# A two-layer transformer block: a fourth half-weight buffer in layer 0's MLP, casts in the order of the products, and modulation rows at 2 turns in 5

## The chip, the core and the metric

One core of a Trainium2 chip runs the whole program in one launch. TensorE (PE) multiplies, VectorE (DVE), ScalarE (ACT) and GpSimd (POOL) do the elementwise work, SyncE (SP) issues nearly all the DMAs, in order, on one queue. The metric is the device time of an execution in microseconds (us). Of the kernel before there are three runs, and one more execution was profiled.

## The reference

The program computes two layers over 512 latent tokens (model width 1024) that are conditioned by a vector c, with 256 context tokens beside them. Layer 0 mixes tokens by windowed grouped-query attention, layer 1 by differential attention, and each is followed by a squared-ReLU MLP of width 4096. Everything is float32.

```python
for i in range(DEPTH):
    mod_x = jax.nn.silu(c) @ w_ada[i] + b_ada[i]
    mod_c = jax.nn.silu(c_ctx) @ w_ada[i] + b_ada[i]
    sh1, sc1, g1, sh2, sc2, g2 = jnp.split(mod_x[:, None, :], N_MOD, axis=-1)
    ...
    x = layer_norm(alpha * x + g1 * ax, ln1_g[i], ln1_b[i])
    fx = sqrelu_mlp(x * (1.0 + sc2) + sh2, mlp_w1[i], mlp_w2[i])   # square(relu(h @ w1)) @ w2
    x = layer_norm(alpha * x + g2 * fx, ln2_g[i], ln2_b[i])
    if need_ctx:      # layer 0 only: the context tokens too
        ...
```

In layer 0 the MLP runs on 768 tokens (latents and context), in layer 1 on 512. The vectors sh, sc and g of both layers are the modulation; their weights, w_ada, are about 50 MB, of which much is loaded and multiplied on DVE while the MLP of layer 0 runs on TensorE.

## The kernel before, in words

**Products.** A float32 weight is split into a high part (ACT casts it to float32r) and a low part (DVE subtracts the high part from the float32 value), and so is each activation. `mm3` (lines 325 to 327) makes a product from three matmuls: high by high, high by low, low by high. So each weight needs a load, a cast on ACT and a subtraction on DVE before TensorE can use it.

**The MLP's first product** (`mlp_pipe`). The 4096 hidden features are taken in pairs of 256, q from 0 to 15. From pair 3 on a pair is done by seven products in place of eight, on quarters of the weights (a scheme like Strassen's). `part_sums` loads the pair's two weight tiles a1 and a2 (tiles `w_raw`, 128 x 1024, from in_w1), whose halves are A11, A12 and A21, A22, has POOL make the sums S1, S2, S3 and S4 from them (`w_sum`, or in place in `w_raw`), and splits A11, A12, A22 and the four sums into high and low parts: `half`, which writes a tile `w_half`, 128 x 1024, the high part left and the low part right. So a pair has seven halves. `weights(q, n)` asks for the first n of them; four of the next pair's are asked for by `ahead` in the middle of a pair, the other three when it starts.

`pair` then runs the products, TensorE in the order A11, A12, S2, S1, S3, S4, A22 (in layer 0 `p3_first` is true). Between them `mix` lets groups of the second product go (`y_groups`, accumulating in `y_ps`, weights `w_h` and `w_l` from in_w2, asked for by `y_weights`; 12 matmuls a group, six from each of two weight tiles). ACT copies a product's result to `relu` and DVE adds to it; product S4 accumulates on the buffer z that the add after S3 (`d3`, DVE `relu<-h_ps`) has to have read first. At a pair's end `squared` makes relu and square on ACT, and the result `hid` is split on ACT and DVE.

**Buffers in layer 0** (`R0`). A half's tile comes from `half_tile`: in turn one of the tiles of the w2 weights' high parts (tag wh), of their low parts (wl), and of the tag bc (two tiles, one of which holds `w_sum`). The ring `rhalf` of 3 says how many may be out. a1 and a2 have one tile each for all pairs, so the next pair's load of a2 waits until A22 is split, that of a1 until S4 is. The tiles `w_raw` of everything else, w2 weights and the modulation's w_ada (`in_w_adaT`), come in turn from NRAW = 3 tiles with the tag raw. Layer 1 (`R1`) has a ring of 4 and tiles of its own.

**Modulation rows.** The generator `filler` (`ada_rows`) does one row block a step: a load of 512 KB from in_w_adaT, then two multiply-and-sum operations on DVE (the CUSTOM operation `w_raw<-w_raw,cB` or `ada_pr<-w_raw,cB`). It has 58 steps. `extra` is called after each y group and once in `ahead`, 13 times in a pair, and takes a step at every third call. What is left at the end of layer 0 is done there. Gates made from them are transposed on TensorE (`gate_t`), copied by ACT (`gate_s`) and written to memory by SP (`gate_d`).

**The order.** Instructions are emitted by a list scheduler (`fl`), which runs the generators of the stages side by side by due times that it keeps itself; a wait in the hardware arises where an emitted instruction needs something later than expected. Each engine takes its instructions in the order emitted; SP's DMAs too, so a load that waits for a tile holds up all those behind it.

Of the kernel before, what the change touches and what calls it, by code (L numbers as in the profile page):

```python
# [15 lines left out]
AF = mybir.ActivationFunctionType  # L16
ALU = mybir.AluOpType
# [217 lines left out]
def hybrid_block(ctx: ExitStack, tc: tile.TileContext, t: dict, out: bass.AP):  # L235
# [460 lines left out]
    def mlp_pipe(l, hx, ready, ntok, acc, get_gates, done, fx, T, R):  # L696
# [40 lines left out]
        def part_sums(q):  # L737
            (a1, g1, f1), (a2, g2, f2) = R.pair_raws()
            q1 = dma(1024, [g1], out=a1, in_=t["w1"][l, 2 * q])
            q2 = dma(1024, [g2], out=a2, in_=t["w1"][l, 2 * q + 1])  # L740
            ws = R.sum_tile()
            (a11, a12), (a21, a22), (s3, s2) = [(x[:, 0:512], x[:, 512:1024]) for x in (a1, a2, ws)]

            def half(src, dep):
                nhalf[0] += 1
                w = R.half_tile(nhalf[0])
                a = ac(512, [dep, R.rhalf.get()], nc.scalar.copy, out=w[:, 0:512], in_=src)
                d = dv(512, [a], nc.vector.tensor_tensor, out=w[:, 512:1024], in0=src, in1=f(w)[:, 0:512],
                       op=ALU.subtract)
                rel = Task()  # L750
                rel.ring = R.rhalf
                return Weight(w[:, 0:512], w[:, 512:1024], d, rel)

            def add(o, x, y, op, deps):
                return gp(pool2(512), deps, nc.gpsimd.tensor_tensor, out=o, in0=x, in1=y, op=op)

            yield half(a11, q1)
            w12 = half(a12, q1)
            yield w12
            e3 = add(s3, a11, a21, ALU.subtract, [q1, q2])  # L760
            e1 = add(a21, a21, a22, ALU.add, [e3])
            e2 = add(s2, a21, a11, ALU.subtract, [e1])
            yield half(s2, e2)
            yield half(a21, e1)
            yield half(s3, e3)
            w = half(a22, q2)
            w.t.ring = f2
            yield w
            w = half(a12, add(a12, a12, s2, ALU.subtract, [e2, w12.t]))
            w.t.ring = f1  # L770
            yield w

        def squared(q, fi, r, d, c):
# [75 lines left out]

        def pair(q, mix, ahead):  # L850
            weights(q, 7 - len(Wp.get(q, [])))
            A11, A12, S2, S1, S3, A22, S4 = Wp[q]
            hid[q] = R.hid_tile(q)
            yield sS.ok
            X, slot = psS("h_ps")[:, 0:nh], sS.take()
# [21 lines left out]
            d3 = dv(nh, [p5, a3], nc.vector.tensor_tensor, out=r1[:, t2], in0=z, in1=r1[:, t2], op=ALU.add)  # L877
            ahead()
            yield from mix(2)
            yield [d3, S4.t if R.p3_first else A22.t]  # L880

            def p3():
                p = product(z, S4, lower(t2, 4), False)
                d = dv(nh, [p, a2], nc.vector.tensor_tensor, out=r0[:, t2], in0=z, in1=r0[:, t2], op=ALU.add)
                sm_.give(zs, d)
                squared(q, 0, r0, [d], slice(0, ntok))

            def p4():
                p = product(X, A22, whole(3), False)
                a = ac(nh, [p], nc.scalar.activation, out=r1[:, t1], in_=X, func=AF.Relu)  # L890
                sS.give(slot, a)
                squared(q, 1, r1, [a, d3], t2)

            if R.p3_first:
                p3()
                yield [a3, A22.t, Tr[3]]
                p4()
            else:
                yield [a3, A22.t, Tr[3]]
                p4()  # L900
                yield [d3, S4.t]
                p3()
            yield from mix(3)

        gates, st, Wy, fresh = [], {}, {}, set()
# [131 lines left out]
        else:  # L1037
# [4 lines left out]
            for _ in sums:  # L1042
                pass
        y_weights(0, 0)
        weights(3, 4)
        y_weights(0, 1, R.ahead)
        yield from steps(2 * ntb)
        for q in range(3, 16):
            if q == R.gate_at:
                gates += yield from get_gates()  # L1050
            if q == 4 and l == 0:
                st2["second"] = True

            def ahead():
                weights(q + 1, 4)
                if q < 14:
                    y_weights((q - 1) // 2, (q - 1) % 2, R.ahead)
                elif l or q == 15:
                    y_weights(6, 1, R.ahead)
                if q == 15:  # L1060
                    R.tail()
                R.extra()
            m = R.mixes[q < 14]
            if q < 15:
                y_weights((q - 2) // 2, q % 2)
            yield from pair(q, lambda i: steps(m[i]), ahead)
# [394 lines left out]
    with tc.tile_pool(name="mlp0", bufs=1, reuse_waits="tile") as pool:  # L1461
# [24 lines left out]
            fl.add(ln_job(pool, acc[tb], tb, hx, A, B, ready, st, r, fx[tb]), 0)  # L1486

        class R0:
            rhalf = Ring(fl, 3)
            mixes = ((2, 2, 2, 0), (4, 4, 4, 0))  # L1490
            p3_first, gate_at, res = True, 16, None
            ahead, done, turn = 1, 0, 0

            def pair_raws(self):
# [3 lines left out]
                return self.ws  # L1498

            def half_tile(self, n):  # L1500
                p_, tag, b = ((wpool, "wh", NH), (wpool, "wl", NH), (pool, "bc", 2))[n % 3]
                return p_.tile([P, 1024], F32R, name="w_half", tag=tag, bufs=b)

            def relu_tile(self):
# [21 lines left out]

            def extra(self):
                self.turn += 1
                if self.turn % 3 == 0:
                    next(filler, None)  # L1530

        def main0():
# [403 lines left out]
    with tc.tile_pool(name="mlp1", bufs=1, reuse_waits="tile") as pool:  # L1936
# [37 lines left out]
        class R1:  # L1974
            rhalf = Ring(fl, 4)
            mixes = ((1, 1, 1, 1), (2, 2, 2, 2))
            p3_first, gate_at, ahead = True, 10, 2

            def pair_raws(self):
                return raw_tile(), raw_tile()  # L1980
# [107 lines left out]
```

## Time and profile before

| | us |
| --- | --- |
| median of three runs (lowest, highest) | 1662.47 (1660.83, 1665.89) |
| the profiled execution's own time | 1666.47 |
| its span, first to last instruction | 1664.6 |
| busy in it: PE / DVE / ACT / POOL | 1574.4 / 1130.1 / 791.4 / 443.1 |
| mean granted TensorE clock | 0.980 |

How to read the rows below: times are microseconds from the start of the span, a row of the timeline has start, duration, engine, line, operation, `out<-in`, and in square brackets the idle time just before it with what ended it; `x2` stands for two equal instructions in a row. Line 260 is the helper of all DVE operations, 264 of ACT's, 268 of POOL's, 275 of SP's loads. In the waits view a line has the waiting instruction, whom it waits for, then the total, the count and the longest. Layer 0's MLP lies from about 330 to 850 us, the border of the layers at 905 to 935.

### The profile page before, as it was taken

How to read it: one execution, taken by the hardware profiler on the slowest of the kernel's cores; microseconds unless marked ns; L12 is line 12 of the kernel's file. 1: busy time of each engine (PE TensorE's matmuls, PEld its weight loads, DVE VectorE, ACT ScalarE, POOL GpSimd, SP SyncE). 2: the span in 40 equal slices, each digit the busy share in tenths (PEclk: the TensorE clock that was granted, in tenths of full speed). 3: DMA queues.
4: the chain of work that ended last, by engine and by line, in shares of the span. 5: the costliest groups of instructions: out<-in, count | busy, mean ns of one | idle time of the engine just before them, and what ended most of it. 6: DMA issues, size and time to landing. Idle time of an engine off the chain costs nothing. (4 is left out here: it accounts for less than half of the span.)

```text
span 1664.6 us, 25124 instructions
## 1 busy us (share of the span) xinstructions
PE 1574.4 (95%) x9465; PEld 1388.4 (83%) x9465; DVE 1130.1 (68%) x2204; ACT 791.4 (48%) x1683; POOL 443.1 (27%) x364
## 2 busy tenths in 40 slices
PE   7899999989899999999998999999989899999997
PEld 5787777789798899889877898999877789999886
DVE  4655677698675668767476777677664975556577
ACT  3465675374343343334316555555541745555550
POOL 1334454105112111121360222220100023323463
PEclk9999999999999999999999999999899999999998
DMA  9111551533454343434323122211114233323321
GB/s 371 42 51 33 178 177 34 189 140 102 134 170 152 127 127 127 137 129 152 123 83 116 62 70 67 71 45 39 48 51 152 87 113 105 100 96 106 95 101 51
DMA packets 66433, 181.16 MB, mean 109 GB/s; under 512 B 7368, under 2 KB 13320, under 8 KB 66312
## 3 DMA queue, kind: packets, MB, share of 16 engines
q1 hardware_dynamic: 66312, 179.56, 32.2%
q8 instruction: 74, 1.21, 0.3%
q14 instruction: 47, 0.39, 0.1%
HBM read 168.49 MB, written 11.04 MB: 108 GB/s over the span
## 5 line engine op out<-in xcount | busy, mean ns | idle before, releaser
L326 PE MATMUL y_ps<-w_l,hid 128*128 128x512 f32 (+1 forms) x648 | 252.5, 390 | 4.9 <-DVE w_l L314 4.9
L325 PE MATMUL y_ps<-w_h,hid 128*128 128x512 f32 (+1 forms) x648 | 252.3, 389 | 1.2 <-DVE g_tmp L583 1.2
L327 PE MATMUL y_ps<-w_h,hid 128*128 128x512 f32 (+1 forms) x648 | 251.5, 388 | 1.0 <-DVE hid L260 1.0
L268 POOL TENSOR_TENSOR w_sum<-w_raw 128x512 f32<-128x512 f32 x52 | 94.9, 1826 | 476.7 <-DMA w_raw<-in_w 402.0
L314 DVE TENSOR_TENSOR w_l<-w_raw,w_h 128x1024 fp32r<-128x1024 f32 (+1 forms) x133 | 163.2, 1239 | 67.5 <-ACT w_h L264 63.4
L264 ACT CAST w_h<-w_raw 128x1024 fp32r<-128x1024 f32 (+1 forms) x133 | 131.0, 998 | 119.1 <-PE y_ps L327 62.2
L327 PEld LDWEIGHTS y_ps<-w_h,hid 128*128 128x128 f32 x648 | 122.2, 189 | 27.3 <-DVE hid L260 1.9
L326 PEld LDWEIGHTS y_ps<-w_l,hid 128*128 128x128 f32 x648 | 122.2, 189 | 27.1 <-DVE w_l L314 5.7
L264 ACT CAST w_half<-w_raw 128x512 fp32r<-128x512 f32 x130 | 79.9, 619 | 132.9 <-PE h_ps L327 76.9
L325 PEld LDWEIGHTS y_ps<-w_h,hid 128*128 128x128 f32 x648 | 122.2, 189 | 23.8 <-DVE g_tmp L583 1.4
L260 DVE TENSOR_TENSOR w_half<-w_raw,w_half 128x512 fp32r<-128x512 f32 x130 | 105.1, 812 | 53.3 <-ACT w_half L264 52.9
L325 PE MATMUL qkv_ps<-w_h,hx 128*128 128x384 f32 (+1 forms) x384 | 128.5, 335 | 0.1
L326 PE MATMUL qkv_ps<-w_l,hx 128*128 128x384 f32 (+1 forms) x384 | 123.7, 322 | 0.2 <-DVE w_l L314 0.2
L327 PE MATMUL qkv_ps<-w_h,hx 128*128 128x384 f32 (+1 forms) x384 | 123.7, 322 | 0.0
L268 POOL TENSOR_TENSOR e<-e,sm 128x512 f32<-128x512 f32 (+2 forms) x96 | 92.6, 977 | 108.7 <-DVE sm L260 90.1
L260 DVE CUSTOM_DVE_ANT_0 w_raw<-w_raw,cB 128x512 f32<-128x512 f32 x112 | 78.4, 728 | 36.6 <-DMA w_raw<-in_w_adaT 36.6
L260 DVE TENSOR_TENSOR fx<-y_ps,fx 128x512 f32<-128x512 f32 x110 | 75.5, 687 | 39.6 <-PE y_ps L327 39.4
L264 ACT ACTIVATE relu<-relu 128x384 f32<-128x384 f32 (+3 forms) x104 | 69.4, 671 | 48.7 <-DVE relu L260 47.4
L268 POOL TENSOR_TENSOR rope<-rope,rope 128x256 f32<-128x256 f32 (+1 forms) x40 | 33.8, 845 | 219.6 <-DVE rope L260 174.9
L325 PE MATMUL h_ps<-hx0m,w_half 128*128 128x384 f32 x208 | 73.5, 353 | 11.5 <-DVE relu L260 11.5
L264 ACT ACTIVATE e<-e,nm 128x513 f32<-128x513 f32 (+2 forms) x96 | 65.9, 688 | 32.9 <-DVE nm L260 26.2
L325 PE MATMUL h_ps<-hx1m,w_half 128*128 128x256 f32 x260 | 73.0, 281 | 3.0 <-ACT relu L264 2.8
(266 smaller groups left out, 4256.4 us busy)
## 6 DMA issues: line engine op xcount, KB each, us to landing
w_raw<-in_w SPq DMA_DIRECT2D x128, 512.0 KB, 3.5
w_raw<-in_w_adaT SPq DMA_DIRECT2D x56, 512.0 KB, 3.8
w_raw<-in_w_ada SPq DMA_DIRECT2D x24, 512.0 KB, 4.3
w_raw<-in_b_w SPq DMA_DIRECT2D x32, 384.0 KB, 3.3
raw<-in_w_ada SPq DMA_DIRECT2D x16, 512.0 KB, 9.3
w_raw<-in_a_wq SPq DMA_DIRECT2D x8, 512.0 KB, 7.7
w_raw<-in_a_wo SPq DMA_DIRECT2D x8, 512.0 KB, 4.3
w_raw<-in_b_wo SPq DMA_DIRECT2D x8, 512.0 KB, 4.8
```

Source lines behind the costliest of these rows:

```text
L260: fn(**kw)
L264: fn(**kw)
L268: fn(**kw)
L314: last["split"] = nc.vector.tensor_tensor(**kw)
L325: nc.tensor.matmul(out=o, lhsT=lh, rhs=rh, start=start, stop=False, **kw)
L326: nc.tensor.matmul(out=o, lhsT=lh, rhs=rl, start=False, stop=False, **kw)
L327: last["pe"] = nc.tensor.matmul(out=o, lhsT=ll, rhs=rh, start=False, stop=stop, **kw)
```

## The change

Four things change, three of them in layer 0 only.

*Sums and casts.* `part_sums` yields S4 before A22, which is the order of the products, so A11, A12, S2, S1, S3, S4, A22 is also the order of the casts; `p3_first` goes, and with it the other order of products, which neither layer used. The sums are made another way: S1 = A21 + A22 into `w_sum`, then S2 = S1 - A11, then S3 = A11 - A21 in place of A21, and S4 = A12 - S2 in place of A12. S2 took three POOL operations before it and takes two now, the first of which needs a2 alone. Layer 1's pairs use this too.

*A fourth buffer.* The ring is 4, and `half_tile` goes in turn through a tile of the tag raw, one of bc, one of wh and one of wl. So every fourth half lies in one of the three tiles through which w2 and modulation weights are loaded.

*w2 weights.* Both tiles of `y_weights(0, 1)` are asked for, ahead of the first halves of pair 3, where one was asked for behind them; both of `y_weights(6, 1)` at pair 15.

*Rows.* `extra` takes a step at 2 calls in 5, where it took one in 3.

```diff
             ws = R.sum_tile()
-            (a11, a12), (a21, a22), (s3, s2) = [(x[:, 0:512], x[:, 512:1024]) for x in (a1, a2, ws)]
+            (a11, a12), (a21, a22), (s1, s2) = [(x[:, 0:512], x[:, 512:1024]) for x in (a1, a2, ws)]
...
-                w = R.half_tile(nhalf[0])
+                w = R.half_tile(nhalf[0] - 1)
...
-            e3 = add(s3, a11, a21, ALU.subtract, [q1, q2])
-            e1 = add(a21, a21, a22, ALU.add, [e3])
-            e2 = add(s2, a21, a11, ALU.subtract, [e1])
+            e1 = add(s1, a21, a22, ALU.add, [q2])
+            e2 = add(s2, s1, a11, ALU.subtract, [q1, e1])
             yield half(s2, e2)
-            yield half(a21, e1)
-            yield half(s3, e3)
+            yield half(s1, e1)
+            yield half(a21, add(a21, a11, a21, ALU.subtract, [e1]))
+            w = half(a12, add(a12, a12, s2, ALU.subtract, [e2, w12.t]))
+            w.t.ring = f1
+            yield w
             w = half(a22, q2)
             w.t.ring = f2
-            yield w
-            w = half(a12, add(a12, a12, s2, ALU.subtract, [e2, w12.t]))
-            w.t.ring = f1
             yield w
...
         y_weights(0, 0)
+        y_weights(0, 1)
         weights(3, 4)
-        y_weights(0, 1, R.ahead)
...
                 elif l or q == 15:
-                    y_weights(6, 1, R.ahead)
+                    y_weights(6, 1)
...
         class R0:
-            rhalf = Ring(fl, 3)
+            rhalf = Ring(fl, 4)
...
             def half_tile(self, n):
-                p_, tag, b = ((wpool, "wh", NH), (wpool, "wl", NH), (pool, "bc", 2))[n % 3]
+                p_, tag, b = ((wpool, "raw", NRAW), (pool, "bc", 2), (wpool, "wh", NH), (wpool, "wl", NH))[n % 4]
...
             def extra(self):
                 self.turn += 1
-                if self.turn % 3 == 0:
+                if self.turn % 5 in (1, 3):
                     next(filler, None)
```

On ACT, around the cast of pair 6's S2 in the middle of pair 5, before: `w_half_5287` is A22 of pair 5, `w_half_5438`, `w_half_5447` and `w_half_5450` are A11, S2 and S1 of pair 6, and the three copies are those of pair 5, the last of them (`relu_5296`) the copy behind its S3, for which S4 of pair 5 waits by way of DVE.

```order
L264 CAST w_half_5438<-w_raw_4058 128x512 [waits DMAHW4_49,PE_49]
L264 CAST w_half_5287<-w_raw_4059 128x512 [waits PE_49]
L264 COPY relu_5295<-h_ps_5294 128x384
L264 CAST w_half_5447<-w_sum_4336 128x512 [waits PE_49,Pool_49]
L264 COPY relu_5296<-h_ps_5294 128x384 [waits DVE_49,PE_49]
L264 CAST w_half_5450<-w_raw_4059 128x512 [waits DMAHW7_49]
L264 ACTIVATE relu_5296<-relu_5296 128x384 [waits DVE_49]
```

After: `w_half_5308` is S4 of pair 5 (its A22 is cast four rows earlier), `w_half_5457`, `w_half_5462`, `w_half_5454` and `w_half_5465` are A12, S2, A11 and S1 of pair 6, and `relu_5316` is the copy behind S3.

```order
L264 CAST w_half_5308<-w_raw_4058 128x512 [waits Pool_49]
L264 COPY relu_5315<-h_ps_5314 128x384 [waits DVE_49,PE_49]
L264 CAST w_half_5457<-w_raw_4058 128x512 [waits DMAHW2_49]
L264 COPY relu_5315<-h_ps_5314 128x384 [waits PE_49]
L264 CAST w_half_5462<-w_sum_4336 128x512 [waits Pool_49]
L264 CAST w_half_5454<-w_raw_4058 128x512 [waits PE_49]
L264 CAST w_half_5465<-w_sum_4336 128x512 [waits DMAHW4_49,DMAHW1_49,DMAHW6_49,DVE_49,Activation_49]
L264 COPY relu_5316<-h_ps_5314 128x384 [waits PE_49]
```

A22 of pair 5 has gone ahead of all of this and no longer waits for TensorE; pair 6's S2 still stands ahead of the copy behind S3, without its wait for TensorE, and now S1 too, behind modulation loads whose raw tile it takes.

On SP, around pair 5, before: tiles 4058 and 4059 are a1 and a2 of the pairs' weights (in_w1), the others are the three raw tiles. Each load waits for DVE alone, which has read what the tile held (the DMAHW waits are for DMA queues).

```order
L275 DMA w_raw_5466<-in_w_adaT 128x2x512 [waits DMAHW1_49,DVE_49]
L275 DMA w_raw_5491<-in_w_adaT 128x2x512 [waits DVE_49]
L275 DMA w_raw_5529<-in_w2 128x1024 [waits DMAHW3_49,DMAHW1_49,DVE_49]
L275 DMA w_raw_4058<-in_w1 128x1024 [waits DMAHW5_49,DVE_49]
L275 DMA w_raw_5596<-in_w_adaT 128x2x512 [waits DMAHW2_49,DVE_49]
L275 DMA w_raw_5647<-in_w_adaT 128x2x512 [waits DMAHW6_49,DMAHW5_49,DVE_49]
L275 DMA w_raw_4059<-in_w1 128x1024 [waits DVE_49]
L275 DMA w_raw_5696<-in_w2 128x1024 [waits DMAHW6_49,DMAHW0_49,DVE_49]
L275 DMA w_raw_5702<-in_w_adaT 128x2x512 [waits DVE_49]
```

After: loads 5434 and 5506 go to raw tiles that held S2 and A22 of pair 5, and wait for TensorE to have used these.

```order
L275 DMA w_raw_5409<-in_w_adaT 128x2x512 [waits DMAHW4_49,DMAHW1_49,DVE_49]
L275 DMA w_raw_5434<-in_w_adaT 128x2x512 [waits PE_49]
L275 DMA w_raw_5468<-in_w2 128x1024 [waits DMAHW5_49,DVE_49]
L275 DMA w_raw_5481<-in_w_adaT 128x2x512 [waits DMAHW7_49,DMAHW6_49,DVE_49]
L275 DMA w_raw_5506<-in_w_adaT 128x2x512 [waits PE_49]
L275 DMA w_raw_5544<-in_w2 128x1024 [waits DMAHW7_49,DVE_49]
L275 DMA w_raw_5605<-in_w_adaT 128x2x512 [waits DMAHW2_49,DMAHW0_49,DVE_49]
L275 DMA w_raw_5656<-in_w_adaT 128x2x512 [waits DMAHW3_49,DMAHW1_49,DVE_49]
```

The w2 tile 5544 for the next y group stands right behind 5506 in the queue.

On SP at the border of the layers, before: the write of the gate (`gate_d15`), made from the last two row loads (8611, 8615), stands ahead of the cosine and sine tables and of lamv.

```order
L275 DMA w_raw_8374<-in_b_w 128x768 [waits DMAHW6_49,DVE_49]
L275 DMA w_raw_8611<-in_w_adaT 128x2x512 [waits DMAHW7_49,DVE_49]
L275 DMA w_raw_8615<-in_w_adaT 128x2x512 [waits DMAHW0_49,DVE_49]
L275 DMA w_raw_8822<-in_b_w 128x768 [waits DMAHW5_49,DVE_49]
L275 DMA w_raw_8828<-in_b_w 128x768 [waits DMAHW6_49,DMAHW1_49,DVE_49]
L275 DMA w_raw_8834<-in_b_w 128x768 [waits DMAHW7_49,DMAHW2_49,DVE_49]
L462 DMA gate_d15_8621<-gate_s_8624 8x128 [waits DMAHW3_49,Activation_49]
L283 DMA c_cosT_8655<-in_cosT 128x256 [waits DMAHW4_49,PE_49]
L283 DMA c_sinT_8657<-in_sinT 128x256
L1607 DMA lamv_8659<-in_lamv 128x256
```

After: there are no row loads here and no gate; both have moved to pair 13.

```order
L275 DMA w_raw_8390<-in_b_w 128x768 [waits DMAHW1_49,DVE_49]
L275 DMA w_raw_8802<-in_b_w 128x768 [waits DMAHW2_49,DVE_49]
L275 DMA w_raw_8808<-in_b_w 128x768 [waits DMAHW3_49,DVE_49]
L275 DMA w_raw_8814<-in_b_w 128x768 [waits DMAHW0_49,DVE_49]
L283 DMA c_cosT_8655<-in_cosT 128x256 [waits DMAHW4_49,PE_49]
L283 DMA c_sinT_8657<-in_sinT 128x256 [waits DMAHW5_49]
L1593 DMA lamv_8659<-in_lamv 128x256 [waits DMAHW6_49]
```

More of the change, by code (lines that the diff above doesn't have):

```diff
@@ L851, in pair @@
             weights(q, 7 - len(Wp.get(q, [])))
-            A11, A12, S2, S1, S3, A22, S4 = Wp[q]
+            A11, A12, S2, S1, S3, S4, A22 = Wp[q]
             hid[q] = R.hid_tile(q)
@@ L879, in pair @@
             yield from mix(2)
[L880 to L902, printed above, removed]
+            yield [d3, S4.t]
+            p = product(z, S4, lower(t2, 4), False)
+            d = dv(nh, [p, a2], nc.vector.tensor_tensor, out=r0[:, t2], in0=z, in1=r0[:, t2], op=ALU.add)
+            sm_.give(zs, d)
+            squared(q, 0, r0, [d], slice(0, ntok))
+            yield [a3, A22.t, Tr[3]]
+            p = product(X, A22, whole(3), False)
+            a = ac(nh, [p], nc.scalar.activation, out=r1[:, t1], in_=X, func=AF.Relu)
+            sS.give(slot, a)
+            squared(q, 1, r1, [a, d3], t2)
             yield from mix(3)
@@ L1488, in hybrid_block @@
         class R0:
-            rhalf = Ring(fl, 3)
+            rhalf = Ring(fl, 4)
             mixes = ((2, 2, 2, 0), (4, 4, 4, 0))
-            p3_first, gate_at, res = True, 16, None
+            gate_at, res = 16, None
             ahead, done, turn = 1, 0, 0
@@ L1976, in hybrid_block @@
             mixes = ((1, 1, 1, 1), (2, 2, 2, 2))
-            p3_first, gate_at, ahead = True, 10, 2
+            gate_at, ahead = 10, 2
             def pair_raws(self):
```

## The prediction

> **What bounds the kernel now.** I read the page first, then PE's waits, then the clock by stages, then, for each wait, the timelines of the engines behind it. The page:
>
> ```profile
> span 1664.6 us, 25124 instructions
> w_raw<-in_w SPq DMA_DIRECT2D x128, 512.0 KB, 3.5
> w_raw<-in_w_adaT SPq DMA_DIRECT2D x56, 512.0 KB, 3.8
> ```
>
> The profiled execution took 1666.47 us, of which 1664.6 is span; the median of the three runs is 1662.47, 4.0 lower, and I subtract the change in the span from either alike. TensorE is busy nearly all the time, so the kernel changes only by what TensorE waits for and by the clock that such a wait costs. Its waits in layer 0's MLP (the window from 300 to 900 us; total, times, longest), and the longest at the border of the layers (window 905 to 935):
>
> ```profile
> PE h_ps L325 <- DVE relu L260: 11.5, 5, 3.4
> PE y_ps L326 <- DVE w_l L314: 4.9, 2, 2.7
> PE y_ps L327 <- DVE hid L260: 1.0, 2, 0.5
> ...
> PE kT_ps L1652 <- DVE sk L260: 7.2, 1, 7.2
> ```
>
> There are few of them. The timeline of PE tells where they are (start, duration, instruction, idle time before it and who ended it):
>
> ```profile
> 428.07 0.50 PE L326 MATMUL y_ps<-w_l,hid 128*128 128x512 f32 x1 [2.24 <-DVE w_l L314]
> ...
> 452.88 0.44 PE L325 MATMUL h_ps<-hx0m,w_half 128*128 128x384 f32 x1 [3.36 <-DVE relu L260]
> ...
> 518.83 0.62 PE L325 MATMUL h_ps<-hx0m,w_half 128*128 128x384 f32 x1 [1.95 <-DVE relu L260]
> ...
> 713.50 0.69 PE L325 MATMUL h_ps<-hx0m,w_half 128*128 128x384 f32 x1 [2.82 <-DVE relu L260]
> ...
> 804.87 0.45 PE L325 MATMUL h_ps<-hx0m,w_half 128*128 128x384 f32 x1 [3.05 <-DVE relu L260]
> ```
>
> The last four are product S4 of pairs 3, 5, 11 and 14: 3.36 + 1.95 + 2.82 + 3.05 = 11.2 us of the 11.5. Each also costs clock. In this view of stretches the number behind the five engines is the granted clock (then DMA share and GB/s):
>
> ```profile
> 425.00:432.00 7.00, 4.76 (x21) 3.62 (x20) 5.82 (x13) 0.59 (x1) 0.00 (x0) 1.00 0.66 217
> 452.00:459.00 7.00, 6.12 (x26) 6.13 (x27) 6.59 (x14) 4.83 (x8) 0.00 (x0) 0.76 0.33 99
> 516.00:524.00 8.00, 6.05 (x25) 5.55 (x25) 6.65 (x10) 4.77 (x8) 0.33 (x1) 0.79 0.16 37
> 712.00:719.00 7.00, 5.50 (x23) 5.51 (x24) 6.66 (x11) 3.60 (x5) 0.00 (x0) 0.76 0.37 136
> 803.00:811.00 8.00, 6.13 (x26) 6.14 (x27) 3.61 (x6) 4.36 (x8) 0.00 (x0) 0.79 0.00 0
> 842.00:849.00 7.00, 5.42 (x18) 4.35 (x18) 3.70 (x4) 0.00 (x0) 7.00 (x6) 0.76 0.19 56
> 910.00:922.00 12.00, 4.83 (x28) 4.48 (x27) 6.21 (x22) 3.46 (x13) 1.45 (x2) 0.72 0.28 88
> ```
>
> Missing clock times length is lost time: 0.24 x 7 or 0.21 x 8 = 1.68 us behind each S4 wait and behind the wait at 842, 0.28 x 12 = 3.36 at the border; nothing behind the 2.24-us wait at 428. The Trainium skill ("TensorE: Matmul & The Clock Gate", What's actually happening) has TensorE fall to half clock after at least one idle window of about 3.4 us; the trace differs, since 1.95 us was enough at 518. By that rule the short waits that I add below would cost no clock and the forecast would be 3.4 us lower.
>
> Why S4 is late in pair 5 (pairs 11 and 14 show the same rows). SP, POOL, ACT and DVE in order of time:
>
> ```profile
> 506.62 0.69 DVE L260 TENSOR_TENSOR w_half<-w_raw,w_half 128x512 fp32r<-128x512 f32 x1
> ...
> 507.34 5.38 SPq L275 DMA_DIRECT2D w_raw<-in_w  x2
> ...
> 512.31 1.30 POOL L268 TENSOR_TENSOR w_sum<-w_raw 128x512 f32<-128x512 f32 x1 [25.35 <-DMA w_raw<-in_w]
> ...
> 515.05 1.28 POOL L268 TENSOR_TENSOR w_sum<-w_raw 128x512 f32<-128x512 f32 x1
> ...
> 516.37 0.62 ACT L264 CAST w_half<-w_sum 128x512 fp32r<-128x512 f32 x1 [11.71 <-POOL w_sum L268]
> 516.89 0.47 ACT L264 COPY relu<-h_ps 128x384 f32<-128x384 f32 x1
> ...
> 518.23 0.55 DVE L260 TENSOR_TENSOR relu<-h_ps,relu 128x384 f32<-128x384 f32 x1
> ```
>
> Half A22 is cast late, because it has to have the buffer of S2 of its own pair (three buffers in turn). Its low part ends at 507.3 and frees the raw tile; the next pair's tile is loaded at 507.34 and lands at 512.3; POOL makes three sums, the third of which is the next pair's S2; ACT, in order, casts that S2 at 516.37 ahead of the copy that this pair's S4 waits for. In pair 3 and at 428 the blocker is another: DVE, in order, sits on a load of modulation weights, with the add that S4 needs, or the low weights that the y group needs, queued behind.
>
> ```profile
> 426.18 0.69 DVE L260 CUSTOM_DVE_ANT_0 ada_pr<-w_raw,cB 128x512 f32<-128x512 f32 x1 [2.63 <-DMA w_raw<-in_w_adaT]
> ...
> 451.65 0.69 DVE L260 CUSTOM_DVE_ANT_0 ada_pr<-w_raw,cB 128x512 f32<-128x512 f32 x1 [3.65 <-DMA w_raw<-in_w_adaT]
> ```
>
> **The change part by part.** *Fourth buffer, product order, two-step S2.* TensorE's own order in the pairs does not change, so only readiness does. With four buffers A22 no longer waits for S2 in pairs 5, 11 and 14 (in pairs 4, 8 and 12 it does), so the next raw tile is free earlier, and S2 needs two sums where it needed three, 1.3 us less (row 515.05); by both, the cast of the next S2 is done before the copy that S4 waits for is due. Gone: the three waits, 1.95 + 2.82 + 3.05 = 7.8, and their clock, 3 x 1.68 = 5.0. If the cover is gone, the same rows come back in pairs 4, 8, 12.
>
> *w2 weights of the first y groups loaded together, and rows paced 2 in 5.* Both shift what stands ahead of the two blocked DVE places. The w2 tile of (0, 1) is now loaded before the rows that blocked it: the 2.24 at 428 goes, and the row loads sit elsewhere at pair 3's S4: 3.36 and its clock 1.68 go. Of the small waits (hid 1.0 and fractions) I take 1.5 as gone, between 0 and 3. Removed in the pairs: 7.8 + 5.0 + 2.24 + 3.36 + 1.68 + 1.5 = 21.6 us.
>
> *What the fourth buffer costs.* It is one of the three raw tiles through which w2 and modulation weights (56 loads) come. A raw tile so far came free when DVE had read it; every fourth half now holds one until its product is done, and SP, in order, waits for that product with all later loads queued behind it. How much does TensorE have to do before it needs what is behind? These are rows of a product (12 matmuls) and of a y group (12), and the DVE groups of the window 300 to 900 (total, mean ns):
>
> ```profile
> 453.33 0.33 PE L327 MATMUL h_ps<-hx0m,w_half 128*128 128x384 f32 x1
> 453.50 0.34 PE L325 MATMUL h_ps<-hx0m,w_half 128*128 128x384 f32 x1
> ...
> 428.64 0.40 PE L325 MATMUL y_ps<-w_h,hid 128*128 128x512 f32 x1
> 428.87 0.40 PE L326 MATMUL y_ps<-w_l,hid 128*128 128x512 f32 x1
> ...
> L260 DVE CUSTOM_DVE_ANT_0 w_raw<-w_raw,cB 128x512 f32<-128x512 f32 x110 | 77.0, 729 | 36.6 <-DMA w_raw<-in_w_adaT 36.6
> L314 DVE TENSOR_TENSOR w_l<-w_raw,w_h 128x1024 fp32r<-128x1024 f32 (+1 forms) x46 | 57.6, 1261 | 16.6 <-ACT w_h L264 12.8 <-PE h_ps L327 3.6
> L260 DVE TENSOR_TENSOR w_half<-w_raw,w_half 128x512 fp32r<-128x512 f32 x65 | 52.3, 808 | 19.3 <-ACT w_half L264 19.2
> L260 DVE TENSOR_TENSOR hid<-relu,hid 128x768 fp32r<-128x768 f32 x32 | 33.4, 1049 | 3.8 <-ACT hid L264 3.5
> ```
>
> Starts are 0.17 us apart in a product (2.1 in all), 0.23 in a y group. When A22 of pairs 5 and 9 (those that lie in a raw tile) ends, SP issues a modulation load and behind it the w2 tile of the next y group. Landing 3.8, two modulation operations 1.46, a half's low part 0.81, a relu add 0.55, then w_l 1.26: 7.9 us. TensorE has two products, 4.2, and seven matmuls of the y group, 1.6: 5.8. A wait of 2.1, twice. When S4 of pairs 4 and 8 ends: landing 3.8, two operations 1.46, two hid 2.1, a low part 0.81, w_l 1.26 = 9.4, less some 0.4 for overlap of following DVE operations, against three products and the seven matmuls, 7.8: 1.2, twice. Every other chain from a product through a raw tile has 2 us or more to spare by the same count. Sum 6.6 us. Clock: the two waits of 2.1 lie near the 1.95 that cost it, 3.4; those of 1.2 get none. Added 10.0. Bounds: none of it, if the landing is shorter by 2; and, if every load lands in 5.0 as the one from 507.34 to 512.31, 1.2 more in all four, with clock in all: 6.6 + 4.8 + 6.7 = 18.
>
> *The border.* The last row loads came behind the last x_spill of layer 0, so on SP the gate's write stood ahead of the cosine table:
>
> ```profile
> 911.13 0.30 SPq L462 DMA_DIRECT2D gate_d<-gate_s  x1
> 911.52 0.33 SPq L283 DMA_DIRECT2D c_cosT<-in_cosT  x1
> ...
> 913.57 0.42 DVE L260 TENSOR_TENSOR rope<-qkv_ps,c_cosT 128x256 f32<-128x256 f32 x1 [1.79 <-DMA c_cosT<-in_cosT]
> 915.37 0.29 DVE L1609 TENSOR_TENSOR lamp<-lamv 128x128 f32<-128x128 f32 x1 [1.37 <-DMA lamv<-in_lamv]
> ```
>
> At 2 in 5, 13 turns a pair give 5.2 loads where they gave 4.3, and the rows end around pair 13; the tables no longer wait for the gate. Late next is the arithmetic: from 913.57 to the sk at which kT starts (917.98, 7.17 us after its predecessor) are 4.4 us, less the 1.37 for lamv: 3.0. So the wait falls from 7.17 to 3.0, and its clock loss from two windows to one: 4.2 + 1.7 = 5.9 saved, between 0 and 7.17 + 3.36 = 10.5.
>
> *The end of layer 0's MLP.* The wait at 842 (2.7, with 1.68 of clock) stays: ACT and DVE are late there under POOL's folds. Two w2 loads stand behind the acc reloads instead of one; I take 0.8, two issues of 0.33 to 0.38, between 0 and one landing of 3.5. Layer 1 takes the new order of casts at nothing: it had four buffers and its S2 wasn't waited for.
>
> Sum: -21.6 - 5.9 + 10.0 + 0.8 = -16.7; the profiled 1666.47 becomes 1649.8, the median 1662.47 becomes **1645.8 us**. With the costs at their bounds: -26.7 to -8.7, so 1636 to 1654.
>
> **The rivals.** *The squeeze of raw tiles is everywhere (slower).* A pair is (713.50 - 518.83) / 6 = 32.4 us and must take 5.2 + 2 loads through the raw tiles, one each 4.5 us. One load holds a tile for 3.8 + 1.46 = 5.3 (rows) or 3.5 + 1 (cast) + 1.26 = 5.8 (w2). So it needs 5.5 / 4.5 = 1.2 tiles on average, and halves leave one to two of three. If they leave fewer than 1.2, DVE sits on a row load once a pair, as at 426 and 451, and TensorE gets a wait of 2.1 with 1.68 of clock in each of the 11 pairs with rows: 41.6, against 26.7 saved: +15, 1677 us. For it: SP is one queue, and the two blocked DVE places were made by just these loads with all three tiles free. Against: the count above finds two bad pairs in four, by at most 2.1.
>
> *The S4 wait moves.* In pairs 4, 8 and 12 A22 still waits for S2, so the next raw tile can be late there: three waits of 2.6 with clock 1.68 come back, 12.8, and 1658. Against: pair 8, whose A22 waits for its S2 today as well, shows no such wait.
>
> *No new waits.* Landings overlap with what DVE does anyway: 10.0 less, 1636. For it: several of the 56 loads show no wait today.
>
> *Nothing comes of it.* The S4 waits go, but TensorE meets the same loads later and the time is given back: 1662.
>
> **How the numbers follow.** The forecast as summed gets 0.58, no new waits 0.12, the moved wait 0.14, nothing 0.06, the squeeze 0.10. About 0.3%, 5 us, can be told from no change, so faster is below 1657.5: 0.58 + 0.12 + half of 0.14 = 0.77; same 0.07 + 0.06 = 0.13; slower 0.10. The range from 1634 to 1659 takes in the bounds and all cases but the last two.
>
> **What would show it.** Right: in the new profile no wait of h_ps on relu above 1 us; clock 1.0 around S4 of pairs 3, 5, 11, 14; y_ps waits on w_l of 1 to 2.5 us just behind pairs 4, 5, 8 and 9 and nowhere else; kT's wait near 3 with no DMA as its cause. Wrong: relu waits in pairs 4, 8 and 12 (the moved wait), w_l waits or DVE waits on in_w_adaT once a pair (the squeeze), or a kT wait of 7 again.

## The result, and the profile after

The change makes the kernel slower, by half a per cent. Seven executions of the changed kernel have a median of 1673.26 us (1668.98 to 1674.61), seven of the kernel before 1662.47 (1660.83 to 1667.39): a ratio of 1.0052 with a 95% interval of 1.0035 to 1.0070. In a later set of runs (e5 below) it was 1.0050 (1.0031 to 1.0069). The forecast was 1645.8, with a range that ended at 1659.

The profiled execution after took 1669.35 us. It lies 3.9 below the median of its kernel, and the one before lay 4.0 above its own; so the two spans differ by 3.0 only, and single profiles show where time goes, while the medians say how much. From the page:

```profile
span 1667.6 us, 25133 instructions
w_raw<-in_w SPq DMA_DIRECT2D x128, 512.0 KB, 3.6
w_raw<-in_w_adaT SPq DMA_DIRECT2D x56, 512.0 KB, 3.9
```

As many loads as before, which land within 0.1 us of the old time. PE's waits in layer 0's MLP (300 to 900 us), and behind them the longest of the window 905 to 935:

```profile
PE y_ps L325 <- ACT w_h L264: 14.2, 3, 9.5
PE y_ps L326 <- DVE w_l L314: 6.7, 7, 2.5
...
PE kT_ps L1638 <- DVE nlam L1601: 3.2, 1, 3.2
```

What was to go went: no line of this window has h_ps waiting for relu (11.5 us before), and kT waits 3.2 where it waited 7.2. In its place y_ps waits for the high parts of w2 weights, 14.2 us where there was no such line, and more often for the low parts (two times before, seven now). The stretches (behind the five engines: clock, DMA share, GB/s) around the old S4 wait of pair 3, the ends of pairs 4, 5 and 9, the layer's end, the border, and the first seven-product pair of layer 1 (pair 16):

```profile
447.00:455.00 8.00, 7.74 (x43) 7.11 (x41) 5.78 (x13) 7.26 (x11) 0.00 (x0) 1.00 0.46 142
485.00:500.00 15.00, 10.52 (x44) 8.55 (x43) 10.66 (x21) 4.82 (x8) 0.37 (x1) 0.89 0.51 174
524.00:532.00 8.00, 6.24 (x28) 5.22 (x29) 6.22 (x14) 1.94 (x3) 0.00 (x0) 1.00 0.66 218
655.00:675.00 20.00, 12.33 (x47) 10.35 (x48) 14.92 (x40) 3.84 (x7) 2.92 (x3) 0.74 0.54 183
838.00:850.00 12.00, 9.49 (x36) 7.32 (x35) 8.74 (x7) 0.00 (x0) 12.00 (x9) 0.86 0.23 78
910.00:935.00 25.00, 19.83 (x130) 18.76 (x129) 15.39 (x44) 13.65 (x37) 5.88 (x6) 0.93 0.31 90
1370.00:1378.00 8.00, 6.02 (x32) 5.72 (x33) 4.14 (x8) 4.96 (x11) 1.28 (x1) 0.79 0.39 132
```

Lost clock, as before one minus the clock times the length, is nothing at 447, 0.11 x 15 = 1.7 behind pair 4, nothing behind pair 5, 0.26 x 20 = 5.2 behind pair 9, 1.7 at the layer's end, 1.75 at the border and 1.7 in pair 16.

**The worst new wait, behind pair 9.** SP, DVE, ACT and PE in order of time:

```profile
650.38 0.88 SPq L275 DMA_DIRECT2D w_raw<-in_w_adaT  x2
...
654.41 0.69 DVE L260 CUSTOM_DVE_ANT_0 ada_pr<-w_raw,cB 128x512 f32<-128x512 f32 x1
...
656.86 0.68 DVE L260 CUSTOM_DVE_ANT_0 w_raw<-w_raw,cB 128x512 f32<-128x512 f32 x1
...
657.58 0.34 SPq L275 DMA_DIRECT2D w_raw<-in_w  x1
...
659.77 0.68 DVE L260 CUSTOM_DVE_ANT_0 w_raw<-w_raw,cB 128x512 f32<-128x512 f32 x1
...
661.11 1.04 ACT L264 CAST w_h<-w_raw 128x1024 fp32r<-128x1024 f32 x1 [6.79 <-DMA w_raw<-in_w]
662.21 0.80 PE L325 MATMUL y_ps<-w_h,hid 128*128 128x512 f32 x1 [9.45 <-ACT w_h L264]
```

SP issues two modulation loads, not one. The first has landed when DVE, done with `hid`, comes to it at 654.41. DVE makes eight modulation operations of them between 654.41 and 660.45, four to a load, with a split and an add in between. The w2 tile goes out at 657.58, just as the fourth operation of the first load (656.86 + 0.68) gives its tile back; it lands 3.5 us later, ACT casts it in 1.04, and TensorE has then stood idle for 9.45. Behind pair 4 a chain of the same kind costs 3.71, again with two row loads ahead of the w2 tile, here of two operations each:

```profile
479.55 0.90 SPq L275 DMA_DIRECT2D w_raw<-in_w_adaT  x2
...
485.12 0.34 SPq L275 DMA_DIRECT2D w_raw<-in_w  x1
...
490.07 0.49 PE L325 MATMUL y_ps<-w_h,hid 128*128 128x512 f32 x1 [3.71 <-ACT w_h L264]
```

### The profile page after: what moved, and what is told of

It reads as the page before. It is cut to its first block, busy times and chain, and to the rows that moved or that the text cites. A ratio compares the mean times of both kernels' runs of the same rounds, so it can differ in the third digit from the quotient of the medians.

```text
span 1667.6 us, 25133 instructions
## 1 busy us (share of the span) xinstructions
PE 1572.0 (94%) x9465; PEld 1385.1 (83%) x9465; DVE 1141.7 (68%) x2204; ACT 790.1 (47%) x1683; POOL 448.2 (27%) x364
## 3 DMA queue, kind: packets, MB, share of 16 engines
q8 instruction: 74, 1.21, 0.3%
## 5 line engine op out<-in xcount | busy, mean ns | idle before, releaser
L325 PE MATMUL y_ps<-w_h,hid 128*128 128x512 f32 (+1 forms) x648 | 254.2, 392 | 15.2 <-ACT w_h L264 14.2
L268 POOL TENSOR_TENSOR w_sum<-w_raw 128x512 f32<-128x512 f32 x26 | 57.6, 2217 | 478.6 <-DMA w_raw<-in_w 330.1
L260 DVE TENSOR_TENSOR w_half<-w_raw,w_half 128x512 fp32r<-128x512 f32 x130 | 101.6, 795 | 39.0 <-ACT w_half L264 38.5
L325 PEld LDWEIGHTS qkv_ps<-w_h,hx 128*128 128x128 f32 x384 | 73.3, 191 | 2.2 <-issue 1.2
```

The costliest lines, as they stand in the source:

```text
L260: fn(**kw)
L268: fn(**kw)
L325: nc.tensor.matmul(out=o, lhsT=lh, rhs=rh, start=start, stop=False, **kw)
```

## The experiments

The first theory, from these rows, was that the loan of a raw tile to every fourth half makes the new waits and the loss. Its rivals: the denser rows cost by themselves, through DVE's time or through their loads; and layer 1 costs something. Every ratio below is to the kernel before on the same chip, with its 95% interval.

**Three buffers (e1).** The changed kernel without the fourth buffer; all else stays.

```diff
-            rhalf = Ring(fl, 4)
+            rhalf = Ring(fl, 3)
...
-                p_, tag, b = ((wpool, "raw", NRAW), (pool, "bc", 2), (wpool, "wh", NH), (wpool, "wl", NH))[n % 4]
+                p_, tag, b = ((wpool, "wh", NH), (wpool, "wl", NH), (pool, "bc", 2))[n % 3]
```

> The changed kernel, but halves of layer 0 go through three buffers as before (w2 high, w2 low, bc), none in a raw tile; new cast order, w2 loading and 2-in-5 rows stay. If the raw tiles lent to halves make the new waits (theory 1), the waits of y_ps on w_h and w_l at pairs 4, 5, 8 and 9 (18.8 us with 6.9 us of clock in the profile of the change) go, some waits of h_ps on relu come back as in the kernel before (up to 11 us and 7 of clock), and the time is 1650 to 1665. If the denser rows make them (theory 2), they stay, with or without the S4 waits: 1673 or more.

1670.99 us, 1.0051 (1.0031 to 1.0071): no better than the whole change. Its waits from 300 to 900:

```profile
PE h_ps L325 <- DVE relu L260: 5.9, 4, 3.5
...
PE h_ps L327 <- DVE w_half L260: 3.3, 3, 1.8
PE y_ps L326 <- DVE w_l L314: 2.9, 1, 2.9
...
PE y_ps L327 <- DVE hid L260: 2.1, 4, 0.7
```

The waits for w_h are gone, so the loan does make them; but others, nearly all for something that DVE makes, stand in their place, and the time is the same. Neither reading of the expectation fits whole. The first theory names the waits and not the cause.

**The fourth buffer elsewhere (e6).** In place of a raw tile, a second tile of the low parts' tag. (A tile of its own, which would have left all others alone, has no room in layer 0: its pool would need 24 KB a partition, and 20.4 are left.)

```diff
-                p_, tag, b = ((wpool, "raw", NRAW), (pool, "bc", 2), (wpool, "wh", NH), (wpool, "wl", NH))[n % 4]
+                p_, tag, b = ((wpool, "wl", NH), (pool, "bc", 2), (wpool, "wh", NH), (wpool, "wl", NH))[n % 4]
```

> The changed kernel, but the fourth buffer of halves is a second one of the tiles of w2's low parts in place of a raw tile (a raw tile holds loads alone). Theory 1 (the raw tile lent to halves keeps loads back): the waits on w_h at pairs 4, 5, 8 and 9 (18.8 us, 6.9 of clock) go; S4 waits stay gone; 1650 to 1660. Rival (the row loads and w2 loads stand in each other's way at 2 rows in 5 whatever the tiles): a wait on w_h of 5 us or more stays at pair 9: 1668 or more.

1672.11 us, 1.0059 (1.0039 to 1.0079). Again no wait for w_h, again others: h_ps for relu 7.5 us, y_ps for hid 4.8 and 2.8, h_ps for w_half 3.8. Which of these two tiles is lent makes no difference to the time.

**Rows at one call in three (e2).** The change, with the rows' old pace.

```diff
-                if self.turn % 5 in (1, 3):
+                if self.turn % 3 == 0:
```

> The changed kernel with rows at one call in three as before; everything else as changed. Theory 1 (raw tiles lent to halves): a w2 tile still comes one load after a row in the only free raw tile, so waits of y_ps on w_h of 3 us and more stay in two pairs of four, though fewer; and the rows again run past the end of layer 0, so kT waits 7 us again: 1668 to 1680. Theory 2 (density): the new waits go and the S4 waits stay gone: about 1650.

1663.24 us, 1.0002 (0.9985 to 1.0019). The loss is gone, although the raw tile is still lent and kT waits 7.6 us again. The waits for w_h in the window fall from 14.2 to 3.7, and a wait of TensorE's gate transposes for modulation sums has come, which neither kernel has:

```profile
PE gate_t L456 <- DVE mods L260: 6.8, 2, 5.4
PE y_ps L326 <- DVE w_l L314: 5.4, 6, 2.2
PE y_ps L325 <- ACT w_h L264: 3.7, 2, 2.1
```

The S4 waits stay gone, as the reading by density had it, but the time is 13 us above its "about 1650": kT's wait is back, the gates wait, and layer 1's price (below) is still in.

**The denser rows alone (e9).** The kernel before with nothing changed but that line: three buffers, no raw tile lent to a half.

```diff
-                if self.turn % 3 == 0:
+                if self.turn % 5 in (1, 3):
```

> The kernel before with rows at 2 calls in 5, nothing else: three buffers, no half in a raw tile. If the rows' density costs by itself (more loads on SP and more operations on DVE ahead of the low weights that TensorE needs), waits of DVE and TensorE grow in the pairs and it is 1668 to 1674, in spite of 5.9 us won at the border. If density only hurts together with a raw tile lent to halves, the pairs lose nothing and the border's gain stays: 1657 to 1661.

1675.93 us, 1.0070 (1.0048 to 1.0091): the rows alone cost as much as the whole change. TensorE's longest waits from 300 to 900 are those for S4, as before (9.4 us for 11.5), and two that the kernel before hardly has:

```profile
PE h_ps L325 <- DVE relu L260: 9.4, 4, 4.2
PE y_ps L327 <- DVE hid L260: 5.4, 5, 1.7
PE h_ps L325 <- ACT w_half L264: 5.0, 2, 3.3
```

How the time is lost is seen between the start of pair 3 and that of pair 10. The stretch, in the kernel before and in e9:

```profile
419.60:650.80 231.20, 222.74 (x1093) 200.33 (x1092) 162.96 (x320) 84.43 (x136) 40.68 (x28) 0.99 0.43 137
```

```profile
420.20:668.70 248.50, 230.40 (x1094) 204.20 (x1093) 182.90 (x374) 85.00 (x136) 41.77 (x28) 0.96 0.45 143
```

The two groups of modulation operations in it (total, mean ns, DVE's idle time before them and who ended it), before and in e9:

```profile
L260 DVE CUSTOM_DVE_ANT_0 w_raw<-w_raw,cB 128x512 f32<-128x512 f32 x62 | 42.0, 706 | 20.7 <-DMA w_raw<-in_w_adaT 20.7
L260 DVE CUSTOM_DVE_ANT_0 ada_pr<-w_raw,cB 128x512 f32<-128x512 f32 x30 | 23.9, 798 | 22.6 <-DMA w_raw<-in_w_adaT 22.1
```

```profile
L260 DVE CUSTOM_DVE_ANT_0 w_raw<-w_raw,cB 128x512 f32<-128x512 f32 x76 | 57.5, 780 | 26.6 <-DMA w_raw<-in_w_adaT 26.6
L260 DVE CUSTOM_DVE_ANT_0 ada_pr<-w_raw,cB 128x512 f32<-128x512 f32 x40 | 31.7, 792 | 20.9 <-DMA w_raw<-in_w_adaT 20.3
```

And the loads that these belong to, before and in e9:

```profile
w_raw<-in_w_adaT SPq DMA_DIRECT2D x32, 512.0 KB, 3.8
```

```profile
w_raw<-in_w_adaT SPq DMA_DIRECT2D x38, 512.0 KB, 3.8
```

The same seven pairs take 17.3 us more. TensorE accounts for all of it: its idle time grows from 231.2 - 222.7 = 8.5 to 18.1, by 9.6, and the clock lost from 0.01 x 231 = 2.3 to 0.04 x 248.5 = 9.9, by 7.6 (each within an us or so, as the clock is rounded). DVE has 6 loads more, 24 modulation operations more, and 182.90 - 162.96 = 19.9 us more work. DVE's own wait for these loads hardly grows, from 20.7 + 22.1 = 42.8 to 46.9. A load is 92 / 32 = 2.9 operations on average, not two. DVE is busy 70% of the time before and 74% after: it is not the bound on average, and yet TensorE loses nearly as much as DVE gets on top. Less the 5.6 us won at the border (kT waits 3.2 here too), 17.3 leaves 11.7; the medians differ by 11.9.

**The same rows, short (e12).** e9 with the modulation operations on 64 of 512 columns, so that seven eighths of those products are left out; the loads are the same 512 KB.

```diff
-                            src = raw[:, i * 512:i * 512 + 512]
+                            src = raw[:, i * 512:i * 512 + 64]
```

(and the same cut of the second operand and the result.)

> The kernel before with rows at 2 calls in 5 (1675.9 us), and each row operation on DVE works on 64 of its 512 columns, so most of the modulation products are left out; all loads stay. The order of loads shifts a little with it. If the density costs through DVE's time (24 more row operations of 0.6 us in pairs 3 to 9 ahead of halves' low parts and hid), the waits in the pairs go: 1650 to 1660. If it costs through the loads themselves (DVE, in order, sits on a row load that has not landed, and SP's queue), most waits stay: 1668 or more.

1658.59 us, 0.9970 (0.9953 to 0.9987), against 1.0070: some 17 us less. The stretch from pair 3 to pair 10, and the operations from 420 to 650:

```profile
421.19:653.04 231.85, 223.95 (x1094) 198.95 (x1093) 121.54 (x372) 84.99 (x136) 39.47 (x28) 0.99 0.48 155
```

```profile
L260 DVE CUSTOM_DVE_ANT_0 w_raw<-w_raw,cB 128x64 f32<-128x64 f32 x76 | 15.5, 239 | 44.3 <-DMA w_raw<-in_w_adaT 44.3
L260 DVE CUSTOM_DVE_ANT_0 ada_pr<-w_raw,cB 128x64 f32<-128x64 f32 x38 | 9.5, 249 | 35.4 <-DMA w_raw<-in_w_adaT 34.8
```

The stretch takes 231.85 us, as in the kernel before (231.20) and not 248.5 as in e9; the 0.3% by which e12 is faster than the kernel before is about what the border gives. Nearly as many operations as in e9, behind the same loads, take 0.24 us in place of 0.78. DVE's idle time on the loads before them, 79 us, has grown with nothing lost by it. So loads that come late for DVE cost nothing where the operations behind them are short: the length of these operations on DVE is what costs. How the two go together is seen at S4 of pair 3, in e9 and in e12:

```profile
450.52 0.69 DVE L260 CUSTOM_DVE_ANT_0 ada_pr<-w_raw,cB 128x512 f32<-128x512 f32 x1 [3.68 <-DMA w_raw<-in_w_adaT]
...
453.71 0.45 PE L325 MATMUL h_ps<-hx0m,w_half 128*128 128x384 f32 x1 [4.22 <-DVE relu L260]
```

```profile
450.45 0.23 DVE L260 CUSTOM_DVE_ANT_0 ada_pr<-w_raw,cB 128x64 f32<-128x64 f32 x1 [3.71 <-DMA w_raw<-in_w_adaT]
...
451.77 0.44 PE L325 MATMUL h_ps<-hx0m,w_half 128*128 128x384 f32 x1 [0.77 <-DVE relu L260]
```

The load is as late in both. In e9 four operations keep the add that S4 needs until 453.10, in e12 until 451.16; the rest of the difference is that TensorE comes there 1.5 us later in e12. Two things stay together in e12 and are not told apart: the work queued on DVE is less, and a short operation gives its raw tile back sooner, by 0.54 us each, so that the next load can leave sooner. And as DVE has less to do in all than in the kernel before, a price of the six added loads that this covers isn't excluded: that would take the kernel before with short operations at the old pace, which was not run.

**Other paces.** Two more, both with layer 1's old order (next experiment): 3 calls in 8 (e10), and 1 in 3 up to call 120, then 1 in 2 (e13).

```diff
-                if self.turn % 5 in (1, 3):
+                if self.turn % 8 in (2, 5, 7):
```

```diff
-                if self.turn % 5 in (1, 3):
+                if self.turn % (3 if self.turn < 120 else 2) == 0:
```

> The changed kernel with rows at 3 calls in 8 and layer 1's sums and casts as before: between one in three and two in five. The rows still end before the border (kT wait near 3 and not 7) and the gates wait less for rows than at one in three (6.5 us there). If the loss grows slowly with density: 1654 to 1658, the fastest. If it is a matter of which loads fall together at pairs 5 and 9, it can be anything from 1655 to 1668, and the wait on w_h at pair 9 tells.

> The kernel that was fastest (rows at one in three, layer 1's sums as before, four buffers; 1660.2), but from about pair 11 on one call in two takes a row, so that the rows end before the border without being denser in pairs 3 to 10. If density costs where the row operations are four to a load (pairs 3 to 10) and not later, the kT wait falls from 7.6 to about 3 at no price: 1653 to 1657. If density costs anywhere, the gain is paid back: 1660 to 1664.

e10: 1671.2 us, 1.0045 (1.0029 to 1.0062). e13: 1670.17 us, 1.0066 (1.0042 to 1.0090). Both lie above every time that was expected of them. In both, kT's wait fell to 3.1 or 3.2, so the border is gained as soon as the rows end before it; and both lose more in the pairs than that against e7 (below), which has the old pace and is otherwise the same, with 12.1 and 10.0 us of waits for w_h. In e13 3.6 of these 10.0 lie in pairs 4 and 5, where the pace is still the old one and e7 has 3.4; the other 6.4 come at 759 and 796, behind the change of pace. Neither pace pays.

**Layer 1's order (e3, e8).** e3 is the change with layer 1's sums and casts as before; e8 the kernel before with layer 1's alone new. The core of e3:

```diff
+            if l:
+                yield half(a11, q1)
+                w12 = half(a12, q1)
+                yield w12
+                e3 = add(s1, a11, a21, ALU.subtract, [q1, q2])
+                e1 = add(a21, a21, a22, ALU.add, [e3])
+                e2 = add(s2, a21, a11, ALU.subtract, [e1])
...
+            A11, A12, S2, S1, S3, S4, A22 = [Wp[q][i] for i in ((0, 1, 2, 3, 4, 6, 5) if l else range(7))]
```

> The changed kernel with layer 1's sums and casts as before the change (order A11, A12, S2, S1, S3, A22, S4, three sums ahead of S2); layer 0 as changed. If the new order of sums in layer 1 makes the 4.0 us wait of its first pair of this kind (sums now run at 1349 us beside DVE's residual operations, which take 2.2 instead of 1.2 us), that wait and 1.7 us of clock go: 5.7 us faster than the change, about 1667. If that wait only shows that TensorE arrives 3.6 us earlier at loads that come no sooner, it stays: 1673.

> The kernel before with layer 1's sums and casts in the new order, nothing else. If the new sums run earlier beside DVE's residual operations and stretch them, the first such pair of layer 1 gets a wait of S4 of 3 to 4 us with 1.7 of clock: 4 to 6 us slower than before, 1667 to 1669. If that wait in the changed kernel came from an earlier arrival of TensorE, there is none here: 1663.

e3: 1665.81 us, 1.0015 (1.0002 to 1.0029), 0.35% less than the change itself. e8: 1661.47 us, 0.9998 (0.9983 to 1.0014), nothing. So layer 1's order costs only together with the changes in layer 0. The profile after shows where: pair 16.

```profile
1348.95 1.21 DVE L672 TENSOR_TENSOR acc<-acc,g1x 128x1024 f32<-128x1024 f32 x1
1349.18 2.13 POOL L268 TENSOR_TENSOR w_sum<-w_raw 128x512 f32<-128x512 f32 x1 [5.92 <-DVE acc L260]
1350.19 2.20 DVE L260 TENSOR_TENSOR acc<-acc,l1b 128x1024 f32<-128x1024 f32 x1
1352.32 2.32 DVE L672 TENSOR_TENSOR acc<-acc,g1x 128x1024 f32<-128x1024 f32 x1
...
1360.83 11.11 SPq L275 DMA_DIRECT2D w_raw<-in_w  x4
...
1367.34 1.05 ACT L264 CAST w_h<-w_raw 128x1024 fp32r<-128x1024 f32 x1 [6.74 <-DMA w_raw<-in_w]
...
1371.98 0.58 PE L325 MATMUL h_ps<-hx1m,w_half 128*128 128x256 f32 x1 [4.04 <-DVE relu L260]
```

POOL's sums run just while DVE updates acc; three updates take 2.2 to 2.32 us in place of 1.21. SP's loads of weights stand behind a transfer that waits for acc (12.1 us in the waits of SP, 9.7 before); the w2 tile is late, ACT sits 6.74 us on its cast, and the copy for S4 is queued behind: 4.04 us and 1.7 of clock. In the kernel before, e8 and e3 that sum runs at 1365.75, 1356.18 and 1364.50, each time behind the last update (which starts at 1357.62, 1349.04 and 1362.54), and the updates take 1.21 to 1.23. Why POOL comes to lie beside them only when layer 0 is changed too is not shown. It is neither the fourth buffer nor the pace: the wait in pair 16 is there with three buffers (e1, 3.11 us) and with the old pace (e2, 3.62), each time beside updates of 2.2 to 2.3. What these two runs keep of the change in layer 0 is the order of sums and casts and the w2 loads.

**What is left when the costs are taken out (e7, e11).** e7 has the edits of e2 and e3: the order of sums and casts, the w2 loads and the fourth buffer in layer 0, with rows at one in three and layer 1 as before. e11 has the edit of e1 too, three buffers.

> The changed kernel with rows at one call in three and layer 1's sums and casts as before the change. If the two losses are separate (rows: 9 to 10 us by the run with rows alone, layer 1: 5.7 to 7.5 by the run with layer 1 alone), it is 1656 to 1659, faster than both kernels by 0.2 to 0.5%. If layer 1's wait was only an earlier arrival, 1663.

> The kernel that was fastest so far (rows at one in three, layer 1's sums as before) with three buffers in place of four. If the fourth buffer pays once the rows are sparse, the S4 waits of pairs 5, 11 and 14 come back in part (3.7 and 1.9 us with clock in the variant with three buffers at 2 in 5) and it is 4 to 10 us slower, 1664 to 1670. If it never pays, because the waits on w_h that it makes at pairs 4 and 5 (5.5 us at one in three) weigh as much, 1658 to 1662.

e7: 1660.17 us, 0.9977 (0.9966 to 0.9988), the best version with the reference's whole work, and faster than both kernels. e11: 1661.66 us, 0.9982 (0.9970 to 0.9994). The intervals overlap almost wholly: the fourth buffer is worth nothing that can be measured, and the gain comes with the order of sums and casts and the w2 loads, which were not run apart. By the profiles the fourth buffer gives and takes: with it (e7) the waits for hid and relu, 5.6 and 2.0 us in e11, are gone, and waits for w_h, 3.4, and of the gate transposes, 6.5, have come, of which e11 has none. The ladder, in this order of steps, is then: order and w2 loads 0.9982, fourth buffer 0.9977, layer 1's order 1.0002 (e2), denser rows 1.0052. The last two steps are +4 and +8 us of medians.

**The change once more (e5)**, for the scatter of single profiles.

> The changed kernel once more, for a second profile. If executions differ by who gets ahead at about 376 us, POOL with the sums of pair 3 or DVE (in the first profile one sum of POOL lasted 21 us there and DVE's operations 0.7 to 1.2; in two variants POOL's sums lasted 2 and DVE's operations nearly 2), a slower execution (1673 to 1675) has the second pattern and is 3 to 6 us late at pair 3. If not, the extra time of a slow execution lies in longer waits at pairs 5 and 9. The waits on w_h at pairs 4, 5, 8 and 9 come again, 15 us or more.

1670.05 us, 1.0050 (1.0031 to 1.0069). Its profile has the waits of the first one almost to the us:

```profile
PE y_ps L325 <- ACT w_h L264: 15.2, 3, 9.7
PE y_ps L326 <- DVE w_l L314: 6.1, 7, 2.5
```

So the new waits are the kernel's own, and not of one execution. POOL's sum of pair 3 takes 21 us here too, so this slower execution (1672.5) isn't told apart by it.

## Why the prediction was wrong, step by step

**Removed in the pairs, 21.6: the waits went, the reasons hold in part.** The S4 waits of pairs 3, 5, 11 and 14 are gone with their clock, and so are the one at 428 and those for hid. The moved wait (pairs 4, 8, 12) didn't come. But the fourth buffer was needed only at the new pace: with three buffers the waits in pairs 5 and 11 are there at 2 in 5 (e1, 3.52 and 1.73 us) and gone at the old pace (e11, where 1.67 in pair 10 is the longest for relu). And the new pace moved neither of the two waits behind blocked DVE places: with it alone (e9) they are still there, 1.62 at 426 and 4.22 in pair 3. That this part came out to the us is in part luck.

**Border, 5.9: right.** 7.17 - 3.2 = 4.0 of wait and 3.36 - 1.75 = 1.6 of clock, 5.6, with the arithmetic as what ends last.

**The layer's end, +0.8: nearly.** The wait of 2.66 is 2.51 and costs the same 1.7 of clock; nothing was added.

**The step that failed: the pace of the rows.** The prediction took the denser rows as a shift ("both shift what stands ahead of the two blocked DVE places") and as a gain at the border, and never priced the work that they put into each pair: 5.2 loads for 4.3, at 2.9 operations each. It counted places where an operand could be late and left DVE's sum out, as DVE was far from full. e9 has only this and loses 0.7%; e12 shortens the operations and loses nothing. In the change it is worth about +8 us net of the 5.6 gained at the border (e2 against the change). It is not the whole miss: e2, at the old pace, is still 17 us above the forecast. There the border isn't won, the gates wait 6.8 us, layer 1 takes its price, and some of the waits for w_h and w_l stay.

**Added by the loan, 10.0: the places right, the size wrong in two of four.** Waits of y_ps came behind pairs 4, 5, 8 and 9, as forecast. Behind 5 and 8 they are 1.84 and 1.17 us, close to the 2.1 and 1.2 of the forecast; behind 4 and 9 they are 4.48 and 9.91, for 1.2 and 2.1. Those for w_h and w_l in the pairs sum to about 18.4 us, from 14.2 + 6.7 less the 2.5 at the layer's end, and cost 1.7 + 5.2 = 6.9 of clock: 25. Three assumptions of the chain failed. It doesn't start at the end of a product: A22 of pair 9 ends near 647 (24 matmuls behind 642.66), but the row loads go out at 650.38, when DVE has made the low part of the w2 tile before; SP's waits around both places are for DVE and for loads, none for TensorE, though it does wait for products elsewhere (19 times, 87.3 us, from 400 to 850). The w2 tile isn't issued right behind the row load: two row loads go first, and behind pair 9 it stood 7.2 us in SP's queue (650.38 to 657.58) until DVE had read the first of them. And a load behind pair 9 brings four modulation operations, 2.8 us, not "two modulation operations 1.46"; behind pair 4 it brings two. But this sum is no price of the loan: with three buffers (e1) other waits cost as much, and with the old pace the loan costs what it gains (e7 beside e11).

**Layer 1 "at nothing": wrong.** The argument was about buffers. The cost, 4.0 + 1.7 in pair 16, comes from when POOL runs. That it runs earlier because the new S1 needs a2 alone is not shown: alone (e8) the same order costs nothing.

By the profiles, -21.6 + 25 - 5.6 + 5.7 = +3.5, against +3.0 of the spans. The medians have some 8 more, which is what the two profiles stand off from their medians; which stages hold that is not shown.

**The rival that came nearest** was the squeeze of raw tiles, 1677. It had the sign, the size and the words "DVE sits on a row load", but its cause isn't the one: with no tile lent e9 loses as much. Whether a raw tile that DVE gives back late, without any loan, has a share in e9's loss is open, as said at e12.

## What to carry to other kernels

Background work on an engine that is 70% busy is not free: before its pace is raised, count the operations per step of it (here 2.9, not 2) and price them as if the engine that waits paid for them, until a run with the work made short says otherwise. A change of several parts hides its own gain; take it apart before it is thrown away or kept: here the order of sums and casts with the w2 loads is worth 0.2%, the fourth buffer nothing, and two parts taken along cost 0.25 and 0.5%. Where a wait is taken away by lending a resource, ask who else goes through it, and price their chain with their own counts.

## What the runs showed of the hardware

**POOL and DVE keep each other out.** First POOL's first sum in the kernel before, in a stretch in which DVE works without a pause; then the same place in e1.

```profile
376.40 21.01 POOL L268 TENSOR_TENSOR w_sum<-w_raw 128x512 f32<-128x512 f32 x1 [23.59 <-DVE acc L260]
```

```profile
375.96 1.94 POOL L268 TENSOR_TENSOR w_sum<-w_raw 128x512 f32<-128x512 f32 x1 [21.62 <-DVE acc L672]
376.66 2.32 DVE L260 TENSOR_TENSOR acc<-acc,g 128x1024 f32<-128x1024 f32 x1
```

An add of 1.3 us (row 512.31 of the prediction) took 21 when it lost, in which time DVE made 26 operations, and 1.94 when it won; then DVE's update took 2.32 for 1.22, and between 372 and 395 TensorE waited 2.85 us for a w_l. In the profiles of e1, e3, e7 and e11 the add takes 1.94 to 6.62, in the other ten 21.0; what decides is not shown. The Trainium skill ("SBUF — State Buffer", SBUF: two separate sides) has a DVE operation with two inputs in SBUF and a GpSimd operation that reads SBUF hold a shared pair of ports exclusively, for a whole instruction; these rows agree, and add that the loser can stand back for many instructions in turn.

**What a wait costs in clock is not fixed by its length.** 3.71 us behind pair 4 cost 1.7 and 9.45 behind pair 9 cost 5.2, while the 1.03 and 0.81 us near 525 cost nothing; before the change 1.95 had cost 1.7 and 2.24 nothing.
